# One matmul for both parts of an operand, and a state-space scan in two blocks of 128 steps

## The chip, the cores and the metric
The kernel runs on one core of a Trainium2 chip. The metric is the device time of one execution in microseconds, the median of three runs. A profile of one more execution was taken.

## The reference
One decoder block over 256 tokens of 2048 features, in float32: a mixer of two parallel branches, merged by sigmoid gates, and a mixture of 32 experts behind it. The parts that matter here:

```python
proj = rms_norm(x) @ w_in            # 2048 -> 512 (s5) + 1536 (lru x) + 1536 (lru y) + 2 * 2048 (gates)
bu = einsum('gpc,blgc->blgp', b_bar, u)                  # s5: 32 groups of 16 inputs, 64 complex states
states = scan(s[t] = lam_bar * s[t-1] + bu[t])           # over the 256 steps
y = real(einsum('gcp,blgp->blgc', c, states)) + d * u    # then gelu, and a sigmoid gate (w_glu)
h = scan(a[t] * h[t-1] + b[t]) * gelu(y_lru)             # lru: a and b from the conv of x_lru, by heads
merged = g_s5 * (out_s5 @ w_proj_s5) + g_lru * (out_lru @ w_proj_lru)
x = x + merged @ w_out               # then the experts, and a final norm
```

## The kernel before, in words
**Layout.** Features stand on the 128 partitions and the 256 tokens on the free axis, so a product of the mixer is a 128 x 256 tile, accumulated over 16 (w_in), 12 (w_plru) or 4 (w_ps5, w_glu) steps of k in one bank of PSUM. To keep float32's precision with the faster fp32r type, weights and activations are split into a high and a low part: `split` (L93) makes `hi` on ScalarE (L99) and `lo = raw - hi` on VectorE (L100), for 1024 columns at a time, and `mm3` (L103) issues three matmuls for each k: hi x hi, hi x lo, lo x hi. The activations' parts are `hT_hi` and `hT_lo` for the normalised input, and `br_hi`, `br_lo` for the branches' outputs (and, before the norm is known, for the raw input).

**Order of the work.** `in_unit` (L398) loads one 128-column unit of w_in (1 MB), splits it in two halves and issues 48 matmuls. The loop at L570 runs over 4 triples of heads: three units for y (GELU, L579), then for each head a unit for x, the head itself (`lru_head`: conv, two small products, gates) and one gate unit (`gate_lru`, tanh on ScalarE, L568). `lru_tail` ends a triple with the scan (L560) and writes `br` (L562, L563). Behind the first two triples stand state-space chunks 0 and 1 (`s5_chunk`, L409), then chunk 2, the last four gate units and chunk 3. Then come 16 units of w_plru (L602), which need the `br` of all heads; 16 units of the s5 gates (L613); the GLU of the state-space output (L624); w_ps5 (L651), whose products are gated (L662), added to the other branch on GpSimd (L663) and split (`merge`, L645: ScalarE, then VectorE L649); and w_out (L726, `mm3w`, 512-column matmuls with their own weight loads). The experts' stage behind it streams 201 MB of weights. The order on each engine is written out by a planner that simulates the program with costs of its own; `high_priority` puts the splits and the evacuations ahead of the state space. On the chip each engine runs its list in order.

**A state-space chunk.** It has four tiles of 128 states (two groups of 64), one after the other in pairs (`SB = 2`). For each tile two matmuls bring the inputs in (L422; 32 rows of contraction, float32, so each is two passes in the trace), at the row tile given by `tile_position`, into one `mid` bank. VectorE turns them by the angle of the step within a block of 16 (L430 to L435), scans all 16 blocks at once (L444), carries between blocks with 16 small instructions (L453 to L475) and adds the carry (L476, L477), scans again, and turns back (L483 to L488). Two matmuls for each tile form the output (L493; 32 columns, at the column tile 32q of the bank `yps[c]`), and L495 adds the skip term.

**Banks.** PSUM has eight: four `acc`, two `mid` (chunks, heads and two of the first y units), two `aux` (`yps` and small products). Of the SBUF pool `mp`, `bz`, `gz` and `st` have two buffers.

Of the kernel before, what the change touches and what calls it, by code (L numbers as in the profile page):

```python
# [35 lines left out]
def block_kernel(  # L36
# [323 lines left out]
    def powers(tc_, ts_):  # L360
# [20 lines left out]
    powers(blk_c, blk_s)
    rho16 = t16("rho16")
    V.tensor_tensor(rho16, rho, rho, op=ALU.mult)
    for _ in range(3):
        V.tensor_tensor(rho16, rho16, rho16, op=ALU.mult)
    d_loc = tb_.tile([P, 16, 16], F32, name="d_loc")
    d_blk = tb_.tile([P, 16, 16], F32, name="d_blk")
    V.tensor_copy(d_loc, rho[:, :, None].to_broadcast([P, 16, 16]))
    V.tensor_copy(d_blk, rho16[:, :, None].to_broadcast([P, 16, 16]))
    V.memset(d_loc[:, :, 0], 0.0)  # L390
    V.memset(d_blk[:, :, 0], 0.0)
# [6 lines left out]
    def in_unit(u, a_hi=hT_hi, a_lo=hT_lo, bank=acc_bank):  # L398
        raw = load_unit(w_in[u], 2048)
        ps = bank()[:, :T]  # L400
# [6 lines left out]
        return ps  # L407

    def s5_chunk(c):  # L409
        yps[c] = aux_bank()  # L410
        SB = 2
        for sb in range(4 // SB):
            bz = mp.tile([P, 2, SB, T], F32, tag="bz", bufs=2, name=nm("bz"))
            gz = mp.tile([P, 2, SB, T], F32, tag="gz", bufs=2, name=nm("gz"))
            s0 = 4 * c + sb * SB
            for i in range(SB):
                s = s0 + i
                q = s % 4
                rows = slice(32 * q, 32 * q + 32)
# [1 line left out]
                for ri in range(2):
                    PE.matmul(ps[:, ri * T:(ri + 1) * T], bt[rows, c, ri, :], uT[rows, c, :], start=True, stop=True,  # L422
                              tile_position=(32 * q, 0))
                p3 = ps.rearrange("p (r j t) -> p r j t", r=2, t=16)
                lc = loc_c[:, s, None, 0:16].to_broadcast([P, 16, 16])
                ls = loc_s[:, s, None, 0:16].to_broadcast([P, 16, 16])
                tt = mp.tile([P, 2, T], F32, tag="st", bufs=2, name=nm("st"))
                ttv = tt.rearrange("p r (j t) -> p r j t", t=16)
                bzv = bz[:, :, i, :].rearrange("p r (j t) -> p r j t", t=16)
                V.tensor_tensor(ttv[:, 0], p3[:, 1], ls, op=ALU.mult)  # L430
                V.tensor_tensor(ttv[:, 1], p3[:, 0], ls, op=ALU.mult)
                V.tensor_tensor(bzv[:, 0], p3[:, 0], lc, op=ALU.mult)
                V.tensor_tensor(bzv[:, 1], p3[:, 1], lc, op=ALU.mult)
                V.tensor_tensor(bz[:, 0, i, :], bz[:, 0, i, :], tt[:, 0], op=ALU.add)
                V.tensor_tensor(bz[:, 1, i, :], bz[:, 1, i, :], tt[:, 1], op=ALU.subtract)  # L435
            d3 = mp.tile([P, SB * T], F32, tag="d3", bufs=1, name=nm("d3"))
            A.activation(d3.rearrange("p (s j t) -> p s j t", s=SB, t=16),
                         d_loc[:, s0:s0 + SB, None, :].to_broadcast([P, SB, 16, 16]), AF.Copy)
            bz4 = bz.rearrange("p r s (j t) -> p r s j t", t=16)
            gz4 = gz.rearrange("p r s (j t) -> p r s j t", t=16)  # L440

            def scan():
                for ri in range(2):
                    V.tensor_tensor_scan(gz[:, ri].rearrange("p s t -> p (s t)"), d3,  # L444
                                         bz[:, ri].rearrange("p s t -> p (s t)"), 0.0, op0=ALU.mult, op1=ALU.add)

            scan()

            w = lambda: mp.tile([P, SB, 16], F32, tag="cw", bufs=8, name=nm("cw"))
            bc, bs = blk_c[:, s0:s0 + SB, 0:16], blk_s[:, s0:s0 + SB, 0:16]  # L450
            gr, gi = gz4[:, 0, :, :, 15], gz4[:, 1, :, :, 15]
            t1, t2, yr, yi, vr, vi = w(), w(), w(), w(), w(), w()
            V.tensor_tensor(yr, gr, bc, op=ALU.mult)  # L453
            V.tensor_tensor(t1, gi, bs, op=ALU.mult)
            V.tensor_tensor(yi, gi, bc, op=ALU.mult)
            V.tensor_tensor(t2, gr, bs, op=ALU.mult)
            V.tensor_tensor(yr, yr, t1, op=ALU.add)
            V.tensor_tensor(yi, yi, t2, op=ALU.subtract)
            fl = lambda t: t.rearrange("p s j -> p (s j)")
            db = fl(d_blk[:, s0:s0 + SB, :])  # L460
            V.tensor_tensor_scan(fl(vr), db, fl(yr), 0.0, op0=ALU.mult, op1=ALU.add)
            V.tensor_tensor_scan(fl(vi), db, fl(yi), 0.0, op0=ALU.mult, op1=ALU.add)
            bc, bs = blk_c[:, s0:s0 + SB, 1:16], blk_s[:, s0:s0 + SB, 1:16]
            v_r, v_i = vr[:, :, 0:15], vi[:, :, 0:15]
            t1, t2, yr, yi = w(), w(), w(), w()
            t1, t2, yr, yi = t1[:, :, 0:15], t2[:, :, 0:15], yr[:, :, 0:15], yi[:, :, 0:15]
            V.tensor_tensor(yr, v_r, bc, op=ALU.mult)
            V.tensor_tensor(t1, v_i, bs, op=ALU.mult)
            V.tensor_tensor(yi, v_i, bc, op=ALU.mult)
            V.tensor_tensor(t2, v_r, bs, op=ALU.mult)  # L470
            V.tensor_tensor(yr, yr, t1, op=ALU.subtract)
            V.tensor_tensor(yi, yi, t2, op=ALU.add)
            rb = rho[:, s0:s0 + SB, None].to_broadcast([P, SB, 15])
            V.tensor_tensor(yr, yr, rb, op=ALU.mult)
            V.tensor_tensor(yi, yi, rb, op=ALU.mult)  # L475
            V.tensor_tensor(bz4[:, 0, :, 1:16, 0], bz4[:, 0, :, 1:16, 0], yr, op=ALU.add)  # L476
            V.tensor_tensor(bz4[:, 1, :, 1:16, 0], bz4[:, 1, :, 1:16, 0], yi, op=ALU.add)  # L477
            scan()
            lc = loc_c[:, s0:s0 + SB, None, 0:16].to_broadcast([P, SB, 16, 16])
            ls = loc_s[:, s0:s0 + SB, None, 0:16].to_broadcast([P, SB, 16, 16])  # L480
            tr = mp.tile([P, SB, T], F32, tag="st", bufs=2, name=nm("so"))
            ti = mp.tile([P, SB, T], F32, tag="st", bufs=2, name=nm("so"))
            V.tensor_tensor(tr.rearrange("p s (j t) -> p s j t", t=16), gz4[:, 1], ls, op=ALU.mult)  # L483
            V.tensor_tensor(ti.rearrange("p s (j t) -> p s j t", t=16), gz4[:, 0], ls, op=ALU.mult)
            V.tensor_tensor(bz4[:, 0], gz4[:, 0], lc, op=ALU.mult)
            V.tensor_tensor(bz4[:, 1], gz4[:, 1], lc, op=ALU.mult)
            V.tensor_tensor(bz[:, 0], bz[:, 0], tr, op=ALU.subtract)
            V.tensor_tensor(bz[:, 1], bz[:, 1], ti, op=ALU.add)  # L488
            for i in range(SB):
                s = s0 + i  # L490
                q = s % 4
                for ri in range(2):
                    PE.matmul(yps[c][32 * q:32 * q + 32, :T], cp[:, s, ri, :], bz[:, ri, i, :],  # L493
                              start=(ri == 0), stop=(ri == 1), tile_position=(0, 32 * q))
# [631 lines left out]
```

## Time and profile before
| | us |
|---|---|
| median of 3 runs (lowest, highest) | 1090.77 (1089.81, 1092.85) |
| the profiled execution | 1093.92 |
| its span, first to last instruction | 1092.1 |
| TensorE (PE) busy | 994.2 |
| VectorE (DVE) busy | 645.6 |
| ScalarE (ACT) busy | 379.1 |
| GpSimd (POOL) busy | 75.6 |

The granted TensorE clock is 0.963 of full speed in the mean. Busy time is the union of an engine's instructions; an instruction's own time is longer than its distance to the next, since they overlap in the pipeline. Stretches are counted from the start of the span.

### The profile page before, as it was taken

What the parts mean: (1) busy time and instruction counts of PE and PEld (TensorE: products, weight loads), DVE (VectorE), ACT (ScalarE), POOL (GpSimd) and SP (SyncE); (2) the same over time, 40 slices, a digit from 0 to 9 for tenths busy, and PEclk for the clock granted to TensorE, in tenths of its full rate; (3) what the DMA queues carried; (4) which work ended last, traced back from release to release, by engine and by line L of the source; (5) the groups of instructions that cost most, each with busy time, mean ns of one, the idle gap of its engine ahead of it and who ended that gap; (6) DMA issues with size and microseconds to landing.
All of it is one profiled execution on the core that took longest, in us unless ns stands there. A gap on an engine that the chain in (4) does not pass through costs nothing. (4 is left out here: it accounts for less than half of the span.)

```text
span 1092.1 us, 18171 instructions
## 1 busy us (share of the span) xinstructions
PE 994.2 (91%) x7435; PEld 749.4 (69%) x7435; DVE 645.6 (59%) x1356; ACT 379.1 (35%) x591; POOL 75.6 (7%) x76
## 2 busy tenths in 40 slices
PE   5999999999999999999999999999988979797872
PEld 5999899998989999998889945445443424343220
DVE  7899999999999964458544433333333312232225
ACT  5568547577633354445434110111110101011102
POOL 4001201223200000006000000000000000000000
PEclk9999999999999999999999999989998989999897
DMA  7655444454244555554979699999999999999991
GB/s 274 212 171 201 155 158 151 157 178 165 97 147 158 184 190 191 193 182 166 392 290 373 247 393 419 375 419 420 419 419 420 419 420 418 420 420 419 420 383 80
DMA packets 45164, 308.93 MB, mean 283 GB/s; under 512 B 5040, under 2 KB 6736, under 8 KB 9744
## 3 DMA queue, kind: packets, MB, share of 16 engines
q1 hardware_dynamic: 44784, 306.84, 72.5%
q8 instruction: 60, 0.98, 0.4%
q0 software_dynamic: 288, 0.85, 0.4%
q14 instruction: 32, 0.26, 0.1%
HBM read 305.57 MB, written 2.10 MB: 282 GB/s over the span
## 5 line engine op out<-in xcount | busy, mean ns | idle before, releaser
L100 DVE TENSOR_TENSOR wlo<-raw,whi 128x1024 fp32r<-128x1024 f32 (+1 forms) x194 | 230.2, 1189 | 98.0 <-ACT whi L99 97.6
L99 ACT ACTIVATE whi<-raw 128x1024 fp32r<-128x1024 f32 (+1 forms) x194 | 197.5, 1022 | 226.8 <-PE acc L105 163.5
L106 PE MATMUL acc<-hT_hi,wlo 128*128 128x256 f32 x848 | 238.8, 282 | 0.0
L105 PE MATMUL acc<-hT_lo,whi 128*128 128x256 f32 x848 | 238.8, 282 | 0.0
L104 PE MATMUL acc<-hT_hi,whi 128*128 128x256 f32 x848 | 238.2, 282 | 0.0
L990 DVE TENSOR_TENSOR once<-acc,once 128x512 f32<-128x512 f32 x128 | 79.8, 685 | 141.0 <-PE acc L986 141.0
L105 PEld LDWEIGHTS acc<-hT_lo,whi 128*128 128x128 f32 x848 | 159.6, 188 | 2.6 <-issue 2.6
L106 PEld LDWEIGHTS acc<-hT_hi,wlo 128*128 128x128 f32 x848 | 159.5, 188 | 2.1 <-issue 2.1
L104 PEld LDWEIGHTS acc<-hT_hi,whi 128*128 128x128 f32 x848 | 159.2, 188 | 2.4 <-issue 2.4
L104 PE MATMUL acc<-br,whi 128*128 128x256 f32 x336 | 95.9, 291 | 8.1 <-ACT br L177 7.7
L105 PE MATMUL acc<-br,whi 128*128 128x256 f32 x336 | 96.8, 290 | 2.4 <-DVE br L178 2.2
L106 PE MATMUL acc<-br,wlo 128*128 128x256 f32 x336 | 96.0, 290 | 2.2 <-DVE wlo L100 2.2
L986 PE MATMUL acc<-ysb,sct 32*128 32x512 f32 x512 | 95.9, 682 | 1.5 <-DVE once L990 0.8
L942 PE MATMUL mid<-eraw,once 128*32 128x512 f32 x512 | 66.0, 632 | 23.8 <-DMA eraw<-in_w_exp_dram 23.8
L918 PEld LDWEIGHTS aux<-sel,x 128*128 128x128 f32 x512 | 61.0, 195 | 31.0 <-issue 20.8
L974 PE MATMUL mid<-eraw,act 128*32 128x512 f32 x504 | 67.8, 658 | 10.2 <-DVE act L955 8.2
L942 PE MATMUL mid<-eraw,xTe 128*32 128x512 f32 x488 | 61.1, 616 | 16.5 <-DMA eraw<-in_w_exp_dram 16.5
L104 PEld LDWEIGHTS acc<-br,whi 128*128 128x128 f32 x336 | 65.7, 198 | 10.0 <-ACT br L177 7.7
L945 ACT ACTIVATE gus<-mid 128x512 f32<-128x512 f32 x32 | 19.1, 597 | 153.6 <-PE mid L942 153.6
L918 PE MATMUL aux<-sel,x 128*128 128x128 f32 x512 | 67.5, 285 | 5.3 <-DVE sct L967 5.3
L105 PEld LDWEIGHTS acc<-br,whi 128*128 128x128 f32 x336 | 66.1, 197 | 4.4 <-DVE br L178 2.7
L106 PEld LDWEIGHTS acc<-br,wlo 128*128 128x128 f32 x336 | 65.8, 197 | 4.0 <-DVE wlo L100 2.4
(352 smaller groups left out, 1307.0 us busy)
## 6 DMA issues: line engine op xcount, KB each, us to landing
eraw<-in_w_exp_dram SPq DMA_DIRECT2D x188, 1024.0 KB, 19.9
raw<-in_w_in_dram SPq DMA_DIRECT2D x59, 1024.0 KB, 4.9
raw<-in_w_out_dram SPq DMA_DIRECT2D x16, 1024.0 KB, 6.3
raw<-in_w_plru_dram SPq DMA_DIRECT2D x16, 768.0 KB, 4.2
raw<-in_w_ps_dram SPq DMA_DIRECT2D x4, 1024.0 KB, 5.0
once<-in_w_exp_dram SPq DMA_DIRECT2D x4, 1024.0 KB, 9.1
xt<-in_xT_dram SPq DMA_DIRECT2D x4, 512.0 KB, 8.7
x<-in_x_dram SPq DMA_DIRECT2D x2, 1024.0 KB, 7.5
```

The lines of the kernel that those rows point to most:

```text
L99: A.activation(hi[:, :n], src, AF.Copy)
L100: V.tensor_tensor(lo[:, :n], src, hi[:, :n].bitcast(F32), op=ALU.subtract)
L104: PE.matmul(ps, whi, ahi, start=first, stop=False)
L105: PE.matmul(ps, whi, alo, start=False, stop=False)
L106: PE.matmul(ps, wlo, ahi, start=False, stop=last)
L918: PE.matmul(pt[:, kk * P:(kk + 1) * P], x1[h][:, k * P:(k + 1) * P], sel[b][:, h].rearrange("p e s -> p (e s)"), start=h == 0, stop=h == 1)
L942: mm = PE.matmul(ps[S * q:S * q + S, :], xT[e // B][:, 4 * j + q, es_], raw[:, q * 512:(q + 1) * 512], start=j == 0, stop=j == 3, tile_pos ...
L945: A.activation(gus[e], ps, AF.Copy)
L974: PE.matmul(ps[S * nb:S * nb + S, :], act[e][:, S * f:S * f + S], raw[:, bank(nb)], start=f == 0, stop=f == 1, tile_position=(0, S * nb))
L986: PE.matmul(sc[nb], sct[e][rows, h, :], ysb[e][rows, :], start=e == ex[0], stop=e == ex[-1], tile_position=(S * nb, 0))
L990: V.tensor_tensor(yacc[h][:, bank(nb)], sc[nb], old[:, bank(nb)], op=ALU.add)
```

## The change
It has these parts:
- `mm2` takes the place of `mm3` for w_in, w_plru and w_ps5. The two parts of the activation are read by one matmul (512 columns, into the two halves of a bank), and the low part of the weight by a second (256 columns, into the first half). The halves are added by `both`, a reduction on VectorE that reads PSUM and writes SBUF, before what reads the product: 88 times (12 y, 12 x, 16 gates, 16 w_plru, 16 s5 gates, 16 w_ps5).
- A chunk handles its four tiles together, in two blocks of 128 steps in place of sixteen of 16. The angles of 128 steps are worked out by six instructions (`fc`, `fs`); one scan per block and part replaces the two rounds; one carry stands between the blocks.
- The input matmuls go two tiles at a time into a tile of two banks (`two_banks`), part outside and state inside; the output ones likewise with four states inside.
- The banks are now four `acc`, one `two` and two `aux`; the heads' product moves from `mid` to `aux`. The pool is closed before the GLU and opened anew with `mid`. In SBUF, `bz`, `gz`, `st`, `d3` have one buffer.

```diff
+    def mm2(ps, whi, wlo, a2, first, last):
+        PE.matmul(ps, whi, a2, start=first, stop=False)
+        PE.matmul(ps[:, :T], wlo, a2[:, 0, :], start=False, stop=last)
+
+    def both(dst, ps):
+        V.tensor_reduce(dst, ps.rearrange("p (w t) -> p t w", w=2), axis=AX.X, op=ALU.add)
...
-    def in_unit(u, a_hi=hT_hi, a_lo=hT_lo, bank=acc_bank):
+    def in_unit(u, a2=hT2, bank=acc_bank):
...
-                mm3(ps, hi[:, cs_], lo[:, cs_], a_hi[k], a_lo[k], k == 0, k == KD - 1)
+                mm2(ps, hi[:, cs_], lo[:, cs_], a2[k], k == 0, k == KD - 1)
...
+        V.tensor_tensor(f4(fc), lc, bc, op=ALU.mult)
+        V.tensor_tensor(tt, ls, bs, op=ALU.mult)
+        V.tensor_tensor(f4(fc), f4(fc), tt, op=ALU.subtract)
+        V.tensor_tensor(f4(fs), ls, bc, op=ALU.mult)
+        V.tensor_tensor(tt, lc, bs, op=ALU.mult)
+        V.tensor_tensor(f4(fs), f4(fs), tt, op=ALU.add)
+        d3 = mp.tile([P, SB, HT], F32, tag="d3", name=nm("d3"))
+        A.activation(d3, rho[:, gs_, None].to_broadcast([P, SB, HT]), AF.Copy)
+        G.memset(d3[:, :, 0], 0.0)
...
+        for i0 in range(0, SB, 2):
+            tt = t4()
+            pair = two_banks()
+            for ri in range(2):
+                for i in (i0, i0 + 1):
+                    rows = slice(32 * i, 32 * i + 32)
+                    at = (i - i0) * 512 + ri * T
+                    PE.matmul(pair[:, at:at + T], bt[rows, c, ri, :], uT[rows, c, :], start=True, stop=True,
+                              tile_position=(32 * i, 0))
+            for i in (i0, i0 + 1):
+                p3 = pair[:, (i - i0) * 512:(i - i0 + 1) * 512].rearrange("p (r j t) -> p r j t", r=2, t=HT)
+                V.tensor_tensor(tt[:, :, i - i0, :].rearrange("p r (j t) -> p r j t", t=HT), p3,
+                                fs[:, None, None, i, :].to_broadcast([P, 2, 2, HT]), op=ALU.mult)
+                V.tensor_tensor(bz[:, :, :, i, :].rearrange("p j r t -> p r j t"), p3,
+                                fc[:, None, None, i, :].to_broadcast([P, 2, 2, HT]), op=ALU.mult)
+            for ri in range(2):
+                o = bz[:, :, ri, i0:i0 + 2, :]
+                V.tensor_tensor(o, o, tt[:, 1 - ri].rearrange("p s (j t) -> p j s t", t=HT), op=ALU.subtract if ri else ALU.add)
+        for j in range(2):
+            for ri in range(2):
+                V.tensor_tensor_scan(f2(gz[:, j, ri]), f2(d3), f2(bz[:, j, ri]), 0.0, op0=ALU.mult, op1=ALU.add)
+            if j == 0:
...
+        for j in range(2):
+            tt = t4().rearrange("p r s t -> p (r s t)").rearrange("p (r s t) -> p r s t", r=2, s=SB)
+            V.tensor_tensor(tt, gz[:, j], fs[:, None].to_broadcast([P, 2, SB, HT]), op=ALU.mult)
+            V.tensor_tensor(bz[:, j], gz[:, j], fc[:, None].to_broadcast([P, 2, SB, HT]), op=ALU.mult)
+            for ri in range(2):
+                o = bz[:, j, ri]
+                V.tensor_tensor(o, o, tt[:, 1 - ri], op=ALU.add if ri else ALU.subtract)
+        for ri in range(2):
             for i in range(SB):
...
+                PE.matmul(yps[c][32 * i:32 * i + 32, :T], cp[:, SB * c + i, ri, :], bz[:, :, ri, i, :],
+                          start=(ri == 0), stop=(ri == 1), tile_position=(0, 32 * i))
...
+            xi = lt("xi")
+            both(xi, ps_in)
...
-        ps = mid_bank()
+        ps = aux_bank()
...
-            A.activation(part[:, d, :], ps, AF.Tanh, bias=hcol(C_BGATE, 16 + d), scale=0.5)
+            both(part[:, d, :], ps)
+            A.activation(part[:, d, :], part[:, d, :], AF.Tanh, bias=hcol(C_BGATE, 16 + d), scale=0.5)
...
+    mixer_banks.close()
+    psum[0] = ctx.enter_context(tc.tile_pool(name="psum2", bufs=1, space=PSUM))
...
-                    mm3(ps, hi[:, cs_], lo[:, cs_], br_hi[k], br_lo[k], k == 0, k == 3)
...
+                    mm2(ps, hi[:, cs_], lo[:, cs_], br2[k], k == 0, k == 3)
+                tg = mp.tile([P, T], F32, tag=("fc", "fs")[dd], name=nm("tg"))
+                both(tg, ps)
+                V.scalar_tensor_tensor(tg, gs5[:, d, :], 1.0, tg, op0=ALU.add, op1=ALU.mult)
```

## Rows read from the trace of the kernel before

**Rows 1.** The page: busy us of each engine, share of the span, instructions

```profile
PE 994.2 (91%) x7435; PEld 749.4 (69%) x7435; DVE 645.6 (59%) x1356; ACT 379.1 (35%) x591; POOL 75.6 (7%) x76
```

**Rows 2.** Stages: length, busy of PE, PEld, DVE, ACT, POOL (instructions), clock, DMA share, GB/s

```profile
45.00:301.00 256.00, 251.95 (x2028) 240.87 (x2027) 248.16 (x595) 168.00 (x258) 43.90 (x36) 1.00 0.48 162
...
45.00:310.00 265.00, 258.77 (x2082) 247.21 (x2080) 257.15 (x611) 171.20 (x263) 43.90 (x36) 1.00 0.48 162
...
310.00:390.00 80.00, 80.00 (x609) 73.99 (x609) 76.42 (x168) 28.22 (x34) 0.00 (x0) 0.98 0.49 159
390.00:482.00 92.00, 92.00 (x769) 90.69 (x769) 42.52 (x38) 43.30 (x52) 0.00 (x0) 1.00 0.56 194
...
488.00:513.00 25.00, 22.41 (x183) 22.04 (x182) 20.52 (x41) 12.06 (x23) 14.78 (x16) 0.99 0.37 127
...
640.00:1065.00 425.00, 370.00 (x2721) 171.20 (x2714) 130.91 (x297) 45.77 (x96) 0.54 (x1) 0.94 1.00 414
```

**Rows 3.** Line L563, the heads' last: ns min/median/max, first and last start

```profile
L563 DVE TENSOR_TENSOR br<-pb,br x12: 392/416/609, 118.0 to 300.5; 128x256 fp32r<-128x256 f32 x12
```

**Rows 4.** Waits of PE up to 620 us: us in total, times, longest

```profile
PE aux L493 <- DVE bz L487: 2.6, 2, 2.2
PE acc L109 <- ACT whi L99: 2.4, 1, 2.4
```

**Rows 5.** Timeline of ACT, s5 gates: start, us, what (fourteen evenly spaced rows, outer two)

```profile
401.34 0.45 ACT L616 ACTIVATE gs<-acc,half_b 128x256 f32<-128x256 f32 x1
...
475.39 0.46 ACT L616 ACTIVATE gs<-acc,half_b 128x256 f32<-128x256 f32 x1
```

**Rows 6.** Timeline of PE, w_out: the first and last of five rows

```profile
521.90 0.39 PE L109 MATMUL acc<-whi,br 128*128 128x512 f32 x1
...
522.81 0.39 PE L110 MATMUL acc<-whi,br 128*128 128x512 f32 x1
```

**Rows 7.** PE: groups of tiled passes in the timeline; then all by form

```profile
341.04 1.12 PE L422 MATMUL mid<-uT,bt 32*128 32x256 f32 x4
...
284.14 1.14 PE L422 MATMUL mid<-uT,bt 32*128 32x256 f32 x8
...
335.89 0.62 PE L493 MATMUL aux<-bz,cp 128*32 128x256 f32 x2
...
337.23 1.06 PE L493 MATMUL aux<-bz,cp 128*32 128x256 f32 x6
...
722.37 1.92 PE L974 MATMUL mid<-eraw,act 128*32 128x512 f32 x16 [0.47 <-DVE act L955]
...
L422 PE MATMUL mid<-uT,bt 32*128 32x256 f32 x64 | 15.8, 400 | 0.0
...
L493 PE MATMUL aux<-bz,cp 128*32 128x256 f32 x64 | 13.9, 396 | 2.6 <-DVE bz L487 2.6
```

**Rows 8.** Timeline of DVE in chunk 3: two 512-column instructions in a row

```profile
358.65 0.69 DVE L483 TENSOR_TENSOR so<-gz,loc_s 128x512 f32<-128x512 f32 x1
359.25 0.69 DVE L484 TENSOR_TENSOR so<-gz,loc_s 128x512 f32<-128x512 f32 x1
```

**Rows 9.** DVE by line and form: busy us, mean ns, idle before

```profile
L444 DVE TENSOR_TENSOR_SCAN gz<-d,bz 128x512 f32<-128x512 f32 x32 | 39.2, 1261 | 0.0
...
L967 DVE COPY sct<-aux 128x256 f32<-128x256 f32 x32 | 13.4, 418 | 0.0
...
L483 DVE TENSOR_TENSOR so<-gz,loc_s 128x512 f32<-128x512 f32 x8 | 5.5, 685 | 0.0
...
L470 DVE TENSOR_TENSOR cw<-cw,blk_s 128x30 f32<-128x30 f32 x8 | 1.5, 183 | 0.0
```

**Rows 10.** Timeline around the end of w_ps5: PE, DVE, PE

```profile
510.04 0.28 PE L106 MATMUL acc<-br,wlo 128*128 128x256 f32 x1
...
511.76 0.41 DVE L662 SCALAR_TENSOR_TENSOR tg<-gs,acc 128x256 f32<-128x256 f32 x1
...
512.71 0.80 PE L109 MATMUL acc<-whi,br 128*128 128x512 f32 x1 [2.39 <-ACT whi L99]
```

More of the change, by code (lines that the diff above doesn't have):

```diff
@@ L64, in block_kernel @@
     units = [mixer_units.enter_context(tc.tile_pool(name="units", bufs=1, reuse_waits="tile")), 4]
-    psum = ctx.enter_context(tc.tile_pool(name="psum", bufs=1, space=PSUM))
+    mixer_banks = ExitStack()
+    psum = [mixer_banks.enter_context(tc.tile_pool(name="psum", bufs=1, space=PSUM))]
     uid = [0]
@@ L73, in acc_bank, with two_banks @@
     def acc_bank():
-        return psum.tile([P, 512], F32, tag="acc", bufs=4, name=nm("acc"))
+        return psum[0].tile([P, 512], F32, tag="acc", bufs=4, name=nm("acc"))
     def mid_bank():
-        return psum.tile([P, 512], F32, tag="mid", bufs=2, name=nm("mid"))
+        return psum[0].tile([P, 512], F32, tag="mid", bufs=2, name=nm("mid"))
+    def two_banks():
+        return psum[0].tile([P, 1024], F32, tag="two", bufs=1, name=nm("two"))
     def aux_bank():
-        return psum.tile([P, 512], F32, tag="aux", bufs=2, name=nm("aux"))
+        return psum[0].tile([P, 512], F32, tag="aux", bufs=2, name=nm("aux"))
     ident = const.tile([P, P], F32, name="ident")
@@ L133, in block_kernel @@
     br_lo = [br[k // 4][:, 1, k % 4, :] for k in range(KD)]
-    hT = [hp.tile([P, KD, T], F32R, name=f"hT_{w}") for w in ("hi", "lo")]
-    hT_hi, hT_lo = ([t[:, k, :] for k in range(KD)] for t in hT)
+    br2 = [br[k // 4][:, :, k % 4, :] for k in range(KD)]
+    hT = hp.tile([P, 2, KD, T], F32R, name="hT")
+    hT_hi, hT_lo = ([hT[:, w, k, :] for k in range(KD)] for w in range(2))
+    hT2 = [hT[:, :, k, :] for k in range(KD)]
     part = hp.tile([P, KD, T], F32, name="part")
@@ L363, in powers @@
         n = 1
-        while n < 16:
+        while n < top:
             bc = tc_[:, :, n:n + 1].to_broadcast([P, 16, n])
@@ L376, in powers @@
             n *= 2
-    powers(loc_c, loc_s)
+    powers(loc_c, loc_s, 16)
     V.tensor_copy(blk_c[:, :, 1], loc_c[:, :, 16])
     V.tensor_copy(blk_s[:, :, 1], loc_s[:, :, 16])
[L381 to L391, printed above, removed]
+    powers(blk_c, blk_s, 8)
+    hop_c = tb_.tile([P, 16], F32, name="hop_c")
+    hop_s = tb_.tile([P, 16], F32, name="hop_s")
+    V.tensor_tensor(hop_c, rho, blk_c[:, :, 8], op=ALU.mult)
+    V.tensor_tensor(hop_s, rho, blk_s[:, :, 8], op=ALU.mult)
     wks.close()
@@ L405, in in_unit @@
                 cs_ = slice(kk * P, (kk + 1) * P)
-                mm3(ps, hi[:, cs_], lo[:, cs_], a_hi[k], a_lo[k], k == 0, k == KD - 1)
+                mm2(ps, hi[:, cs_], lo[:, cs_], a2[k], k == 0, k == KD - 1)
         return ps
+    SB, HT = 4, T // 2
     def s5_chunk(c):
         yps[c] = aux_bank()
[L411 to L415, printed above, removed]
-            for i in range(SB):
-                s = s0 + i
-                q = s % 4
-                rows = slice(32 * q, 32 * q + 32)
-                ps = mid_bank()
[L421 to L494, printed above, removed]
@@ new lines, in s5_chunk @@
+        gs_ = slice(SB * c, SB * c + SB)
+        fc = mp.tile([P, SB, HT], F32, tag="fc", name=nm("fc"))
+        fs = mp.tile([P, SB, HT], F32, tag="fs", name=nm("fs"))
+        t4 = lambda: mp.tile([P, 2, SB // 2, T], F32, tag="st", name=nm("st"))
+        tt = t4().rearrange("p r s t -> p (r s t)")[:, 0:SB * HT].rearrange("p (s j t) -> p s j t", s=SB, t=16)
+        f4 = lambda f: f.rearrange("p s (j t) -> p s j t", t=16)
+        sh = [P, SB, HT // 16, 16]
+        lc, ls = (l[:, gs_, None, 0:16].to_broadcast(sh) for l in (loc_c, loc_s))
```

54 lines of the change are left out of this document (35 added, 19 removed).

## The prediction, made blind
> **What bounds the kernel now.** I read the page first, then the stages, then the waits, then single instructions. TensorE is busy in 91% of the span [rows 1]. The table by stage [rows 2] cuts the span where the work changes. From 45 to 310 us the input matmuls of the conv and gate units run, with the recurrence's heads and the first state-space chunks beside them: TensorE is busy for 258.8 of 265 us, but VectorE for 257.2 too. Up to 301 us, where the last head has written the operand of the next stage [rows 3], VectorE has 248.2 of 256. So the first stage has two full engines. From 310 to 390 (w_plru) TensorE is full and VectorE at 76 of 80, because chunks 2 and 3 of the state space are worked off there; from 390 to 482 (s5 gates) TensorE is full and VectorE at 42.5 of 92. The stage of w_ps5 (488 to 513) has VectorE at 20.5 of 25. From 640 to 1065 the experts run at a DMA share of 1.00 and 414 GB/s: that stage lasts as long as its bytes, so whatever the mixer gains or loses moves it as a block. After the start TensorE hardly waits in the mixer: two waits of L493 for VectorE, 2.6 us together, and one of 2.4 us for ScalarE ahead of w_out are among the longest [rows 4].
>
> **Matmuls in pairs of parts.** A step of k is three 256-column matmuls now; it becomes one of 512 columns over both parts and one of 256. An s5-gate unit is 48 of the old matmuls, and its evacuations follow each other by 74.05 us in 13 steps [rows 5], 5.70 us a unit, so 118.7 ns a matmul. The 512-column ones of w_out, also with a weight load each, follow each other by 0.91 us in 4 steps [rows 6]: 227 ns. A step costs 356 ns now, and 227 + 119 = 346 ns after: 10.4 ns saved, from which I take that each matmul has a fixed part. 56 input units of 16 steps, 16 w_plru units of 12 and 16 w_ps5 units of 4 are 1152 steps: **-12.0 us**, of which 6.7 lie in the 40 units before w_plru, 4.7 in w_plru and the s5 gates, 0.7 in w_ps5. The bounds: nothing, if 512 columns cost twice 118.7, and -18 us, if the 256-column matmul beside it also falls by some 5 ns. The row is the nearest there is: same operand type, same weight load.
> The Trainium skill ("TensorE: Matmul & The Clock Gate", section "Wait — 56ns, not 53.3ns?") puts the fixed cost of a warm matmul at about 2.5 ns, by which 1152 matmuls fewer would save an estimated 2.9 us; the rows above say 10.4 ns a step.
>
> **State-space matmuls.** The input side (L422) stands on row tiles. A group of four passes takes 1.12 us, and where the order happened to bring two states into two banks, eight passes take 1.14 us [rows 7]. The 64 passes are 12 groups of four and 2 of eight, 15.7 us. After: 8 groups of eight, 9.1 us, **-6.6 us**. The output side (L493) is a group of two (0.62 us) and one of six (1.06 us) for each half chunk, 8 x 1.68 = 13.4 us. With the part outside and the state inside, four column tiles go at once: sixteen 512-column passes of that kind take 1.92 us [rows 7], and 256 columns should take some 1.1 us, 1.4 if the group is cut in two. Four groups: 4.4 to 5.6 us, **-8.5 us**. Together 15.1, of which about 9.5 before 310 us (two and a half chunks).
>
> **VectorE.** Instructions overlap: two 128x512 ones start 0.60 us apart though each is busy 0.69 [rows 8, 9], so I count busy time less 0.09. Half a chunk now: 12 of 256 columns (0.33, as L967), 4 scans (1.17, L444), 18 small (0.1, as L470), 6 of 512 (0.60, L483), in all 14.1 us; a chunk 28.6 with its last addition. After: 6 instructions for the tables, 12 to turn in, 4 to turn out, all of 512 (13.2), 4 of 1024 (4.6), 4 scans (4.7), the carry (0.5), the last addition: 23.4. A chunk saves 5.2 us. The tables of constants lose 14 small instructions and gain 2, -1.3 us.
> Against that stand 88 new reductions (`both`), 512 columns from PSUM to 256. No row shows one. Bounds: 0.42 us, if outputs count (a 256-column copy from PSUM, L967), 1.26 us, if each element passes twice as in the scan (L444) [rows 9]. I take 0.69 busy, 0.60 net, the row of 512 elements read once (L483), since a reduction reads 512. The ScalarE readers then read SBUF, at the same cost.
> First stage, up to the last head: 248.2, less 10.4 (two chunks), less 1.3, plus 40 x 0.60 = 24, less about 9.7 for chunk 2's share there, which can be put off into w_plru: 250.8, and with the 7.8 us in which VectorE idles now, 258.6. The last head would be done at 303.6. TensorE by itself would be through at 310 - 6.7 - 9.5 = 293.8. So VectorE decides there, and **+10 us** of TensorE's saving is lost, between 0 (the idle time shrinks, chunk 1 is put off too) and 16 (chunk 2 is not put off). Behind it, from 310 to 482, VectorE had 118.9 us; it gets 9.7 + 32 x 0.60 = 29 more and 10.4 less, 138 of the some 162 TensorE needs: covered by the s5 gates, where VectorE idles half the time.
>
> **w_ps5.** For one d VectorE now has half a split (0.57), one addition and one merge (0.33 each), 1.23 us against TensorE's 1.42; it gets 0.60 more and becomes the longer one, 29.3 us for 16 d against 22. Now its last L662 starts at 511.76, 1.7 us after TensorE's last matmul there, and w_out's first matmul at 512.71 waits behind the merges on ScalarE [rows 4, 10]. w_out needs two free banks, so the evacuation of the 14th d: about 14 x 1.83 + 2 = 27.6 us after the start (2 for the first product), where 16 x 1.42 and the wait of 2.4, 25.1 us, are taken now. With w_out's first splits queued behind these on VectorE I take **+4 us**, between 0 and 10.
>
> **Banks and queues.** The mixer's banks are closed before the GLU, so its first matmul waits for the last reduction of the s5 gates: **+1.3 us** (0.69 and two hand-overs), 0 to 3. A head's product moves from a `mid` bank to an `aux` bank, and a chunk's output holds the other: the second head of a triple waits until the chunk is done, where before it waited for the chunk's last `mid` bank. I cost that at nothing: TensorE has gate and conv units to go on with; without them it would be 2 to 5 us. One `two` tile instead of two `mid` banks makes the second pair wait for four reads, 2.4 us, under matmuls of other units. The memset on POOL queues behind the heads' products there, VectorE's scan behind it: four times, under 1 us each, at nothing. No DMA is added, SP's queue is unchanged.
>
> **The sum**: -12.0 - 15.1 + 10 + 4 + 1.3 = -11.8 us. The profiled execution took 1093.92 us with a span of 1092.1, so 1082.1 after; the median of the runs shown is 3.2 below it, 1090.77 - 11.8 = **1079 us**.
>
> **Rivals.** (a) VectorE does not bind: reductions nearer 0.42, or the order hides more. For it: VectorE's state-space work has slack until the GLU, at 482. Then some -26: 1065 us. Against: 248 of 256 us now.
> (b) The 512-column matmul is no cheaper. Then TensorE is through with the first stage at 300.5, still under VectorE's 303.6, and only the 5.4 us behind it are lost: -6.4, 1084 us. Against: the rows at 227 ns. By the 2.5 ns that the Trainium skill gives ("TensorE: Matmul & The Clock Gate", the section above) the time would be near this.
> (c) VectorE becomes the bound of the whole mixer, slower than before. One mechanism: the reduction's own time, in the first stage and w_ps5. 56 of them lie where VectorE decides, so -11.8 turns to zero at 0.21 us more each, a reduction of 0.90 us. At the scan's 1.26 us it is 56 x 0.57 = 32 more: +20, 1111 us. For it: no reduction of this shape is in the trace, and its pairs lie 1 KB apart. Against: all elementwise rows cost the same per element, from PSUM or SBUF.
> The Trainium skill ("TensorEngine Tiling (Array Packing)", section "PSUM Bottleneck") warns of just this side: tiling speeds up TensorE and not the evacuation, which may become the bottleneck.
> (d) It all cancels: chunk 2 is not put off and w_ps5 costs 8: near 1090. That the tiles don't overlap as said is excluded by the rows of eight passes.
>
> **How the numbers follow.** My forecast, 1070 to 1087: 0.46. (a) 0.15. (b) lies with the forecast's upper part, 0.07 beside it. (d) 0.14, (c) 0.18. The measurement tells 0.3%, 3.3 us, from no change. Faster: 0.46 + 0.15 + 0.05 = 0.66 (a little of (b) ends within 0.3%), same 0.16, slower 0.18. The range leaves out half of (c) and the end of (a): 1062 to 1096.
>
> **What would show it.** Right: 512-column matmuls 227 ns apart; an s5-gate unit 5.53 us; groups of eight at 1.14 us and of sixteen near 1.1; reductions of 0.69 us; VectorE without gaps up to about 300 us and TensorE waiting there for some 10 us; w_out starting 5 us or more behind the last w_ps5 matmul. Wrong: TensorE as full as now before w_plru (then (a)), reductions of 0.9 us or more (then (c)), or an expert stage that does not keep its length.

## The result, and the profile after

The changed kernel takes **1126.0 us** (1123.6 to 1128.4) against 1091.8 for the kernel before on the same chip: a ratio of 1.031, 95% interval 1.028 to 1.034. The forecast was 1079, its range ended at 1096. The profiled execution took 1128.4 with a span of 1126.7 us.

The page's busy times, and the stages (length; busy of PE, PEld, DVE, ACT, POOL; clock, DMA share, GB/s), to be held against [rows 1, 2]:

```profile
PE 990.9 (88%) x6283; PEld 695.6 (62%) x6283; DVE 674.2 (60%) x1252; ACT 372.2 (33%) x581; POOL 70.1 (6%) x80
...
45.00:341.00 296.00, 263.04 (x1484) 222.73 (x1483) 286.42 (x566) 165.60 (x255) 39.43 (x40) 0.93 0.43 147
341.00:409.00 68.00, 62.15 (x352) 53.48 (x351) 54.49 (x78) 27.12 (x32) 0.00 (x0) 0.95 0.51 172
409.00:501.00 92.00, 92.00 (x526) 80.67 (x525) 52.44 (x51) 40.98 (x48) 0.00 (x0) 1.00 0.57 191
...
275.00:300.00 25.00, 15.94 (x81) 12.38 (x80) 25.00 (x45) 13.46 (x23) 5.66 (x5) 0.76 0.36 116
325.00:350.00 25.00, 15.17 (x74) 12.47 (x75) 24.10 (x44) 10.65 (x17) 5.16 (x6) 0.73 0.23 66
```

The last head, and the chunks' ends (ns min/median/max, first and last start), against [rows 3]:

```profile
L561 DVE TENSOR_TENSOR br<-pb,br x12: 392/408/413, 177.2 to 340.9; 128x256 fp32r<-128x256 f32 x12
...
L490 DVE SCALAR_TENSOR_TENSOR uT<-uT,prm,aux x4: 464/468/481, 194.2 to 364.8; 128x256 f32<-128x256 f32 x4
```

The waits of PE from 45 to 410 us (us in total, times, longest), against [rows 4]:

```profile
PE acc L114 <- DVE part L119: 13.7, 4, 6.4
PE aux L108 <- ACT xh L533: 6.1, 1, 6.1
PE acc L114 <- DVE pl L119: 5.3, 1, 5.3
PE two L453 <- DVE bz L459: 4.9, 1, 4.9
PE acc L115 <- DVE wlo L104: 3.2, 4, 1.8
```

The last head comes at 340.9 us in place of 300.5, with VectorE busy for 286.4 of the 296 us before it and TensorE waiting, most of all for the reductions (L119). Between 275 and 300 us VectorE fills all 25 us and TensorE 15.9, at a mean granted clock of 0.76. The four chunks, by contrast, end earlier, at 364.8 against 395.6. The s5 gates run at full TensorE again (92 of 92), but their end has moved, and w_out's first matmul stands at 537.9 in place of 512.7 [rows 10]:

```profile
L122 PE MATMUL acc<-whi,br x160: 278/389/632, 537.9 to 640.6; 128*128 128x512 f32 x96, 128*128 128x256 f32 x64
```

The parts that the change is made of, one by one. Reductions (with the counts of the whole kernel), steps of `mm2`, tiled groups, and the tanh of the s5 gates:

```profile
L119 DVE TENSOR_REDUCE part<-acc x26: 657/678/691, 58.1 to 339.2; 128x256 f32<-128x512 f32 x26
L119 DVE TENSOR_REDUCE gs<-acc x16: 690/691/692, 417.1 to 501.4; 128x256 f32<-128x512 f32 x16
...
419.75 0.40 PE L114 MATMUL acc<-hT,whi 128*128 128x512 f32 x1
419.98 0.28 PE L115 MATMUL acc<-hT,wlo 128*128 128x256 f32 x1
420.10 0.40 PE L114 MATMUL acc<-hT,whi 128*128 128x512 f32 x1
...
126.86 1.13 PE L453 MATMUL two<-uT,bt 32*128 32x256 f32 x8
...
191.83 1.07 PE L488 MATMUL aux<-bz,cp 128*32 128x256 f32 x16
...
L620 ACT ACTIVATE gs<-gs,half_b x16: 493/494/497, 418.0 to 502.3; 128x256 f32<-128x256 f32 x16
```

A reduction takes 0.68 to 0.69 us, eight and sixteen tiled passes 1.13 and 1.07 us: as forecast. An s5-gate unit takes 84.3 / 15 = 5.62 us, where 5.53 were forecast and 5.70 were there before. None of this explains 35 us; the question was where they come from.

### The profile page after: what moved, and what is told of

Same layout as the page of the kernel before. It is cut to its first block, busy times and chain, and to the rows that moved or that the text cites. A ratio compares the mean times of both kernels' runs of the same rounds, so it can differ in the third digit from the quotient of the medians.

```text
span 1126.7 us, 15795 instructions
## 1 busy us (share of the span) xinstructions
PE 990.9 (88%) x6283; PEld 695.6 (62%) x6283; DVE 674.2 (60%) x1252; ACT 372.2 (33%) x581; POOL 70.1 (6%) x80
## 5 line engine op out<-in xcount | busy, mean ns | idle before, releaser
L114 PE MATMUL acc<-hT,whi 128*128 128x512 f32 x848 | 307.5, 402 | 12.8 <-DVE part L119 7.3
L103 ACT ACTIVATE whi<-raw 128x1024 fp32r<-128x1024 f32 (+1 forms) x194 | 197.0, 1022 | 237.6 <-PE acc L114 139.8
L115 PE MATMUL acc<-hT,wlo 128*128 128x256 f32 x848 | 243.1, 288 | 2.7 <-DVE wlo L104 2.7
L114 PEld LDWEIGHTS acc<-hT,whi 128*128 128x128 f32 x848 | 163.1, 193 | 51.8 <-ACT pb L587 5.1
L115 PEld LDWEIGHTS acc<-hT,wlo 128*128 128x128 f32 x848 | 163.5, 193 | 5.5 <-DVE wlo L104 4.5
L114 PE MATMUL acc<-br,whi 128*128 128x512 f32 x272 | 99.4, 407 | 16.4 <-DVE part L119 6.4
L114 PEld LDWEIGHTS acc<-br,whi 128*128 128x128 f32 x272 | 52.7, 194 | 30.2 <-issue 15.8
L995 PEld LDWEIGHTS acc<-ysb,sct 32*128 32x128 f32 x512 | 40.7, 194 | 35.3 <-issue 26.7
L986 ACT ACTIVATE ysb<-mid 128x512 f32<-128x512 f32 x32 | 19.1, 597 | 129.8 <-PE mid L983 129.8
L122 PE MATMUL acc<-whi,br 128*128 128x512 f32 (+1 forms) x160 | 57.0, 357 | 1.5 <-DVE tg L119 1.5
L124 PE MATMUL acc<-wlo,br 128*128 128x512 f32 (+1 forms) x160 | 55.4, 359 | 2.2 <-DVE wlo L104 2.2
```

Of the source, the lines that this page charges most:

```text
L103: A.activation(hi[:, :n], src, AF.Copy)
L114: PE.matmul(ps, whi, a2, start=first, stop=False)
L115: PE.matmul(ps[:, :T], wlo, a2[:, 0, :], start=False, stop=last)
L995: PE.matmul(sc[nb], sct[e][rows, h, :], ysb[e][rows, :], start=e == ex[0], stop=e == ex[-1], tile_position=(S * nb, 0))
```

## The experiments

The theories at the start: **A**, the heads' product shares the `aux` banks with the constants' transposes and the chunks' outputs and comes late (the first head's tanh is at 132 us, at 86 before); **B**, VectorE is full, and every reduction ahead of the last head delays it; **C**, `pl` (the reduced w_plru product) sits in the chunks' single `fc` and `fs` buffers, so w_plru can't be evacuated while a chunk is under way. Later came **D**, the place of chunks 2 and 3 in VectorE's order. Times of whole kernels are medians, beside runs of the kernel before (1093.6 to 1094.8 us in these comparisons); a stage or a place in the span comes from the one profiled execution of each kernel. A miss is a time outside the range of the theory under test.

### The two halves of the change alone

`e2_mm2_only`: two-part matmuls and reductions put into the kernel before. `e3_s5_only`: the changed kernel without them:

```diff
     def mm2(ps, whi, wlo, a2, first, last):
-        PE.matmul(ps, whi, a2, start=first, stop=False)
-        PE.matmul(ps[:, :T], wlo, a2[:, 0, :], start=False, stop=last)
+        mm3(ps[:, :T], whi, wlo, a2[:, 0, :], a2[:, 1, :], first, last)
...
-            both(xi, ps_in)
```

> The kernel before with the two-part matmuls and their 88 reductions alone: old state space, old banks with the heads in mid. Theory A (banks): the heads start early as before, at some 82 us; VectorE is loaded by 40 x 0.6 = 24 us more before the last br without the 12 us that the new chunks save, so the last br comes some 15 to 20 us later than 300 and the time is 1095 to 1110 us, faster than the changed kernel. Theory B (VectorE): worse than the changed kernel, 1130 us or more, since VectorE lacks the saving of the new state space.

> The changed kernel with three matmuls per step again and no reductions: new state space and new banks alone. Theory A (banks): most of the loss stays, the first head starts near 130 us, the last br comes after 325 us, time 1105 to 1120 us. Theory B (VectorE): VectorE has 5 us less per chunk than before and no reductions, so the last br comes before 300 us and the time is 1075 to 1088 us.

Measured: e2 **1120.7 us**, ratio 1.025 (1.019 to 1.031); e3 **1084.4 us**, 0.992 (0.990 to 0.995). Their first stages up to the last head, and the last head, e2 first, then e3:

```profile
45.00:325.70 280.70, 264.51 (x1431) 219.95 (x1430) 268.42 (x623) 170.35 (x258) 38.65 (x36) 0.96 0.44 149
...
L577 DVE TENSOR_TENSOR br<-pb,br x12: 409/413/426, 133.2 to 325.4; 128x256 fp32r<-128x256 f32 x12
```

```profile
45.00:301.30 256.30, 251.38 (x2084) 243.64 (x2083) 248.15 (x503) 162.55 (x255) 50.75 (x40) 1.00 0.50 167
...
L553 DVE TENSOR_TENSOR br<-pb,br x12: 409/413/417, 165.0 to 301.0; 128x256 fp32r<-128x256 f32 x12
```

The loss is in the two-part matmuls. In e2 the last head is 25 us late, what 40 reductions take (24 us); its time is a miss for both theories, between 1110 and 1130. In e3 the heads are in `aux` as in the changed kernel, and their first tanh is at 118 us, yet the last head is on time: theory A falls. B holds in kind. But e3 gains only 9 us, and its last head is no earlier than before, though VectorE has less to do for a chunk: by 301 us it has already worked off almost all of chunk 2 (it ends at 307, at 340 before).

### The heads' bank

```diff
-        ps = aux_bank()
+        ps = acc_bank()
         for w in range(2):
```

> The changed kernel with one edit: the heads' product takes an acc bank in place of an aux bank. Theory A (banks): the heads queue in the aux banks behind the transposes of the constants and behind the chunks' outputs, so the first head starts at 130 us in place of 82 and the last br is written at 341 us in place of 300. Then the first head should start near 85 us, the last br come at 305 to 315 us and the time fall by 20 to 30 us, to 1096 to 1106 us. Theory B (VectorE is full with the 88 reductions, whatever the banks): the last br stays at 330 us or later, and the time at 1120 us or more.

> The changed kernel with two edits: the heads' product in an acc bank, and the reduced w_plru product in two buffers of its own in place of the chunks' fc and fs. Theory C: because fc and fs have one buffer each, w_plru's evacuation can't begin before chunk 3 is done, so the chunk can't lie under w_plru and the s5 gates. Then this kernel is faster than the one with the heads' product in an acc bank alone by 3 us or more, and chunk 3 ends after the first w_plru evacuation. If the tag does not matter the two agree within 1 us.

Measured: **1184.4 us**, 1.085 (1.079 to 1.091), and **1184.0 us** with `pl` in own buffers as well (its diff stands further below). Both are misses, for A and for C; only B's "1120 us or more" holds, and B has no reason for so much. Chunks' ends, the last head and the longest waits of the first:

```profile
L490 DVE SCALAR_TENSOR_TENSOR uT<-uT,prm,aux x4: 449/474/480, 154.3 to 282.8; 128x256 f32<-128x256 f32 x4
...
L561 DVE TENSOR_TENSOR br<-pb,br x12: 409/414/958, 158.1 to 395.0; 128x256 fp32r<-128x256 f32 x12
...
PE two L453 <- DVE bz L459: 27.5, 4, 10.9
PE acc L108 <- ACT xh L533: 26.8, 11, 6.2
PE aux L488 <- DVE bz L485: 18.0, 2, 9.3
```

With the heads out of `aux`, the written order has all four chunks ended at 282.8, and the last head comes 54 us later still, at 395.0. TensorE's order has chunk matmuls and heads close behind their operands, and TensorE waits for them 72.3 us in these three rows. So the `aux` bank had not delayed the heads. That it had held the chunks back, and that this had helped, is inferred from the order and has no run of its own; by amount e1 has only 7.5 us more chunk work ahead of its last head than the changed kernel (96.3 against 88.8), so most of the 54 us are waits. This is what led to D. Theory C could not show here, since no chunk is left when w_plru starts.

### Reductions only behind, or only ahead of, the last head

```diff
-    def in_unit(u, a2=hT2, bank=acc_bank):
+    def in_unit(u, a2=hT2, bank=acc_bank, mm=mm2o):
...
-        ps = in_unit(28 + d)
+        ps = in_unit(28 + d, mm=mm2)
```

`mm2o` is `mm3` with `mm2`'s operands; this is `f2_mm2_late` (w_ps5 has `mm2o` too). `f3_mm2_early` has it the other way round.

> The changed kernel with the two-part matmuls only in w_plru and the s5 gates, where VectorE has room; three matmuls per step elsewhere, w_ps5 among it. Theory B: the 56 reductions ahead of the last head and in w_ps5 make the whole loss, the 32 others are hidden. Then the time is that of the new state space alone (1084.4 us) less up to 4.7 us: 1079 to 1085 us. If the reductions cost wherever they stand: 1090 us or more.

> The changed kernel with the two-part matmuls only in the 40 units ahead of the last head; three matmuls per step in w_plru, the s5 gates and w_ps5. Theory B: the 40 reductions there keep most of the loss: the last br at 330 to 341 us, and 1112 to 1126 us. If the loss sits in w_plru (evacuation tied to chunk 3) or in w_ps5: below 1105 us.

Measured: f2 **1099.4 us**, 1.003 (1.000 to 1.006), a miss; f3 **1122.2 us**, 1.023 (1.020 to 1.026), as B says. f2's first stage equals e3's (last head at 301.2), but then TensorE waits, and the first product of w_plru is used at 334.6 us (L615):

```profile
PE acc L114 <- DVE pl L119: 16.6, 1, 16.6
...
L615 DVE SCALAR_TENSOR_TENSOR part<-part,pl x16: 417/424/426, 334.6 to 388.5; 128x256 f32<-128x256 f32 x16
```

The first reduction of w_plru writes into `fc`, which the chunk still needs. That is C.

### Holding chunks 2 and 3 back

`f1_chunks_late` (on the changed kernel) and `f4_late_both` (on f2); `pl` in `fc` and `fs` makes sure that a chunk can't start before the unit ahead of it:

```diff
-    s5_chunk(2)
...
-    s5_chunk(3)
     for d in range(KD):
...
+        if d in (1, 8):
+            s5_chunk(2 if d == 1 else 3)
```

> The changed kernel with chunks 2 and 3 moved behind the second and the ninth unit of w_plru; they reuse the buffers of the reduced w_plru products, so they can't start before. Theory D (order): in the changed kernel chunk 2 and most of chunk 3, some 40 us of VectorE, stand ahead of the last head; only 24 of the 40 us by which the last br is late are the 40 reductions. Then the last br comes at 300 to 312 us, the chunks are hidden by w_plru and the s5 gates, and the time is 1090 to 1103 us. Theory B alone (reductions): the last br stays within 8 us of 341 and the time within 8 us of 1126. Rival: the chunks don't end before the GLU, and the loss turns up there; then the last br is early and the first matmul of w_out still later than 525 us.

> The kernel with two-part matmuls only in w_plru and the s5 gates, and with chunks 2 and 3 moved behind the second and the ninth unit of w_plru. Theory D: VectorE is then relieved of some 20 us before the last head, TensorE decides there, and the last br comes at 285 to 297 us in place of 301; time 1065 to 1080 us, the fastest so far. If the order does not matter: as with the chunks where they were, within 3 us.

Measured: f1 **1128.0 us**, 1.029 (1.026 to 1.032); f4 **1104.4 us**, 1.008 (1.005 to 1.011). Both times are misses, though the last head moves nearly as D says, from 340.9 to 313.7 and from 301.2 to 291.9. What was gained is given back in w_plru: f1's w_out starts at 542.2 us, as late as the rival said, but not for its reason, since the chunks end at 406.5, ahead of the GLU. f1's wait in w_plru:

```profile
PE acc L114 <- DVE pl L119: 25.0, 2, 14.2
```

### Both repairs together

`pl` gets two buffers of its own; where chunks are held back, only units 0 and 11 share `fc`, with the chunks behind them:

```diff
-        pl = mp.tile([P, T], F32, tag=("fc", "fs")[d % 2], name=nm("pl"))
+        pl = gsp.tile([P, T], F32, tag="pl", bufs=2, name=nm("pl"))
```

> Two-part matmuls only in w_plru and the s5 gates, as in the run that gave 1099.4 us, with the reduced w_plru product in two buffers of its own. There TensorE waited 16.6 us in one piece for the first reduction of w_plru, which may only write into fc when the last chunk is done with it. Theory C (the shared buffers): this wait goes, the first w_plru evacuation comes at 306 us in place of 335 and the time falls by 12 to 20 us, to 1079 to 1087 us. If the reductions themselves were the cost: within 4 us of 1099.

> As the previous kernel, with chunks 2 and 3 held back behind the first and the twelfth unit of w_plru (those two units alone share the chunk's buffer). With the chunks held back before, the last br came at 291.9 us in place of 301.2, but TensorE waited 26.7 us for the shared buffers. Theories C and D together: last br near 292 us, no wait above 5 us in w_plru, time 1068 to 1078 us. If holding the chunks back only moves the load: 1079 to 1087 us, as the previous kernel.

> The changed kernel with the reduced w_plru product in two buffers of its own, nothing else. Theory C: the first w_plru evacuation comes right behind the last br (341 us) in place of 359, TensorE's wait of 5.3 us goes, and the time falls by 8 to 15 us, to 1111 to 1118 us. If the buffers don't matter there, since chunk 3 is nearly done by then: within 3 us of 1126.

> The changed kernel, two-part matmuls everywhere, with both repairs: w_plru's reduced product in its own buffers but for the first and the twelfth unit, behind which chunks 2 and 3 are held back. Theories C and D: the last br near 314 us, no long wait in w_plru, the time 1095 to 1105 us; what then remains against the kernel before is the 40 reductions ahead of the last head (24 us, less the saving of the chunks) and w_ps5. If the time stays above 1115 us, the reductions of w_plru and the s5 gates are not hidden after all.

Measured:

| | mm2 in | `pl` own | chunks 2, 3 late | us | ratio to before | last head | w_out starts |
|---|---|---|---|---|---|---|---|
| the changed kernel | all | no | no | 1126.0 | 1.031 (1.028 to 1.034) | 340.9 | 537.9 |
| g3 | all | yes | no | 1115.6 | 1.019 (1.015 to 1.022) | 340.4 | 530.6 |
| g4 | all | yes | yes | 1100.6 | 1.007 (1.004 to 1.010) | 312.6 | 510.4 |
| g1 | w_plru, s5 gates | yes | no | 1073.9 | 0.981 (0.979 to 0.984) | 301.1 | 493.6 |
| g2 | w_plru, s5 gates | yes | yes | **1069.9** | 0.979 (0.977 to 0.982) | 288.1 | 490.7 |

g2, g3 and g4 came within their expected ranges, g1 5 us below its range. In g1 the wait of 16.6 us is gone, and the first product of w_plru is used at 308.6 us, 26 us earlier than in f2:

```profile
L615 DVE SCALAR_TENSOR_TENSOR part<-part,pl x16: 391/409/419, 308.6 to 373.2; 128x256 f32<-128x256 f32 x16
```

Last head and first stage of g4, then of g2:

```profile
L561 DVE TENSOR_TENSOR br<-pb,br x12: 405/408/411, 176.9 to 312.6; 128x256 fp32r<-128x256 f32 x12
...
45.00:313.00 268.00, 247.78 (x1429) 212.76 (x1428) 254.38 (x513) 162.96 (x253) 42.40 (x39) 0.97 0.47 162
```

```profile
L562 DVE TENSOR_TENSOR br<-pb,br x12: 408/414/954, 165.1 to 288.1; 128x256 fp32r<-128x256 f32 x12
...
45.00:288.00 243.00, 240.52 (x2002) 234.21 (x2001) 225.40 (x467) 157.24 (x249) 49.07 (x39) 1.00 0.50 170
```

In g2 TensorE is full up to the last head (240.5 of 243) and VectorE is not (225.4). It is the fastest kernel of the study, though its interval and g1's overlap. What VectorE had to do for the chunks ahead of the last head, in the changed kernel (45 to 341.3 us) and in g4 (45 to 313 us); columns: count, busy us, mean ns, idle before:

```profile
L467 DVE TENSOR_TENSOR_SCAN gz<-d,bz 128x512 f32<-128x512 f32 x14 | 19.0, 1383 | 0.0
L457 DVE TENSOR_TENSOR st<-two,fs 128x512 f32<-128x512 f32 x16 | 10.8, 676 | 0.0
...
L485 DVE TENSOR_TENSOR bz<-bz,st 128x512 f32<-128x512 f32 x12 | 9.3, 813 | 0.0
...
L481 DVE TENSOR_TENSOR st<-gz,fs 128x1024 f32<-128x1024 f32 x6 | 7.3, 1211 | 0.0
```

```profile
L467 DVE TENSOR_TENSOR_SCAN gz<-d,bz 128x512 f32<-128x512 f32 x8 | 10.9, 1396 | 0.0
...
L485 DVE TENSOR_TENSOR bz<-bz,st 128x512 f32<-128x512 f32 x8 | 6.2, 812 | 0.0
...
L457 DVE TENSOR_TENSOR st<-two,fs 128x512 f32<-128x512 f32 x8 | 5.4, 680 | 0.0
...
L481 DVE TENSOR_TENSOR st<-gz,fs 128x1024 f32<-128x1024 f32 x4 | 4.9, 1213 | 0.0
```

The whole kernel has 16 of the scans, 16 of L457, 16 of L485 and 8 of L481. In the changed kernel all four chunks have been turned in, and three turned out, before the last head; in g4 two chunks and no more. Over all lines of `s5_chunk`, each instruction counted from the end of the one before it, that is 88.8 us of VectorE against 50.7, and the kernel before had 71.8 there. The 38 us less bring the last head 28 us earlier, not 38: VectorE's busy time falls by 32.0 us, since other work takes some of the place, and it idles for 4.0 us more (13.6 of 268, 9.6 of 296).

### The price of a reduction, and w_ps5

On g4: `h1_ps5_mm3` has `mm3` and no reduction in w_ps5, `h2_twice` does each of the 40 early reductions twice, `h3_half` lets ScalarE copy one half:

```diff
+    def half(dst, ps):
+        A.activation(dst, ps[:, :T], AF.Copy)
+        V.tensor_tensor(dst, dst, ps[:, T:], op=ALU.add)
...
-            both(xi, ps_in)
+            half(xi, ps_in)
```

> The repaired changed kernel (1100.6 us) with three matmuls per step and no reductions in w_ps5. If w_ps5's reductions cost what the prediction said, 4 us between 0 and 10: 1092 to 1099 us, and the wait of TensorE between its last w_ps5 matmul and w_out shrinks. If w_ps5 costs nothing: within 2 us of 1100.6.

> The repaired changed kernel with each of the 40 reductions ahead of the last head done twice. Theory B (VectorE decides there, one for one): 40 x 0.6 = 24 us more, 1118 to 1130 us, with the last br some 24 us later than 314. If another wait decides there: under 10 us more.

> The repaired changed kernel where ScalarE copies the first half of the 40 products ahead of the last head out of PSUM and VectorE adds the second half, 256 columns in place of a reduction over 512. Theory B: VectorE saves about 0.27 us each, 11 us, and the time is 1086 to 1094 us. Rival: the extra hand-over between ScalarE and VectorE ahead of each head costs as much as it saves: 1097 to 1108 us.

Measured: h1 **1090.7 us**, 0.997 (0.995 to 0.999); h2 **1123.0 us**, 1.026 (1.021 to 1.030); h3 **1097.6 us**, 1.004 (1.002 to 1.006). h2's last head, then h3's first stage:

```profile
L562 DVE TENSOR_TENSOR br<-pb,br x12: 407/410/415, 186.8 to 332.6; 128x256 fp32r<-128x256 f32 x12
```

```profile
45.00:312.60 267.60, 245.56 (x1397) 210.33 (x1396) 239.26 (x506) 178.42 (x293) 41.92 (x39) 0.96 0.46 156
```

h2: 40 more reductions make the last head 20.0 us later and the time 22.4 us longer, 0.56 us each. h3 takes 15 us of busy time off VectorE (239.3 against 254.4), and the last head stays where it was (312.2 against 312.6): VectorE now idles instead, in kind what the rival with the extra hand-over said. So in g4 the amount of VectorE's work alone no longer sets the last head; that the hand-over takes its place is not shown. h3's w_out even starts 4.8 us later than g4's (515.2 against 510.4), so its shorter time comes from behind that point.

h1 is 10.0 us faster than g4, a little beyond the 9 allowed. From the last tanh of the s5 gates to w_out's first matmul it needs 32.8 us (477.4 to 510.2) and g4 35.6 (474.8 to 510.4): w_ps5's reductions account for 2.8 us there. But since h1's last head is 3.7 us later (316.3), the two start w_out together, and the whole difference of the profiles lies behind it, where h1 takes 578.1 us and g4 592.8, although the code is the same (g4's profiled execution, 1104.9, was 4.3 us above its median). In f3, which has no reductions in w_ps5 either, this stretch is 590.4, in the kernel before 579.4, in g2 575.4. In g4 the DMA share is 0.77 between 670 and 710 us, in h1 0.97. Three stretches of 5 us in g4, in the columns of [rows 2]:

```profile
680.00:685.00 5.00, 5.00 (x14) 2.00 (x12) 0.69 (x1) 0.00 (x0) 0.00 (x0) 0.67 1.01 421
685.00:690.00 5.00, 5.00 (x13) 2.52 (x10) 1.29 (x2) 0.00 (x0) 0.00 (x0) 0.50 0.63 262
690.00:695.00 5.00, 4.64 (x18) 2.62 (x20) 2.45 (x6) 0.22 (x1) 0.00 (x0) 0.50 0.00 0
```

TensorE's granted clock falls to half while the engine is busy, and only then do the transfers stop. Just ahead of the fall and in it stand groups of passes with 32 rows of contraction (L994, four at 679.7 and eight at 682.2 us). The same dip, a mean clock of 0.79 and a DMA share of 0.77 in 40 us, stands in e2, f3 and h2, the three other kernels that need 590 us or so behind w_out's start (589.9 to 591.3); the changed kernel has a weaker one (0.91 and 0.90), and in g2 both are 1.00. The written order of TensorE's instructions in that stretch differs between these kernels. Whether that is the cause was not tried.

## Why the prediction was wrong

**The failed step** is in the paragraph on VectorE: "less about 9.7 for chunk 2's share there, which can be put off into w_plru". The forecast left some 52 us of chunk work ahead of the last head (71.8, less 10.4 and 9.7). In the changed kernel it was 88.8: chunk 2 was not put off, and most of chunk 3 came ahead of the last head too. The prediction's bound for that, 16 us, took the order of before as the worst case. By this account the 37 us more are the 37.3 us by which the last head comes later than forecast (340.9, not 303.6). g4 holds the chunks back: 50.7 us of chunk work there, the last head at 312.6, the time 15.0 us below g3. That bears out most of it, 28 us; the 9 us by which g4's last head is still later than 303.6, with no more chunk work than forecast, are other work of VectorE and 13.6 us of idle time where the forecast had 7.8. From the last head to w_out's first matmul the sum held, 197.3 us forecast (303.6 to 512.7 - 11.8) and 197.0 measured, but in part by luck: TensorE idles for 5.9 of the 68 us behind the last head, which was not foreseen, and finds chunk matmuls done that the forecast had placed there. What is left of the 47 us is 9.4 us behind w_out's start (588.8 against 579.4), the stretch whose cause is open.

**Not seen at all**: `pl` in the single buffers `fc` and `fs`. The prediction relied on chunks 2 and 3 being covered by w_plru and the s5 gates; with this tag they can't be, as w_plru's first reduction waits until the chunk is done with the buffer. Own buffers are worth 10.4 us on the changed kernel (g3), and 25.5 on f2 (g1); up to w_out's first matmul the profiles show 7.3 and 17.8 us of that (511.4 in f2). Holding the chunks back pays only with them: 1128.0 with shared buffers, 1115.6 with own ones alone, 1100.6 with both.

**VectorE's costs** were right: reductions at 0.69 busy and 24.4 us for 40 (24 forecast), a chunk at 24.1 us (96.3 for the four in e1, 23.4 forecast). So was what follows from them in kind, TensorE waiting for VectorE ahead of the last head. The reductions cost about what they take: the last head is 20.0 us later in h2, 25 in e2. That they would fit beside the saving on the chunks was not true even with chunks 2 and 3 behind the last head: g4 is at 1.007, its last head 12.1 us later than before.

**Two-part matmuls**: -12.0 forecast. The step is 351 ns (5.62 / 16), 512 columns 0.23 us and 256 columns 0.12; 5 ns a step saved, not 10.4, so 5 to 6 us for 1152 steps. The Trainium skill ("TensorE: Matmul & The Clock Gate", section "Wait — 56ns, not 53.3ns?") gives 2.5 ns for a matmul's fixed part; the saving here lies between that and the forecast. Even so they do no harm where VectorE has room: g1, with 32 reductions behind the last head, is at 0.981 and e3, without them, at 0.992. In the two profiles g1 is 3.8 us ahead at w_out's first matmul (493.6 against 497.4); 448 steps by 5 ns would be 2.3. The rest of the 10 us between the medians is not explained.

**State-space matmuls**: the groups took 1.13 and 1.07 us, as forecast; e3, with them and the new chunk, gains 0.8%, and its w_out starts 15.3 us earlier than before (497.4).

**w_ps5**: +4 forecast, 2.8 us measured up to w_out, up to 10.0 with the open part. The sign given for it did not come: w_out's first matmul is 1.8 us behind w_ps5's last (536.1 to 537.9), not 5 or more, as TensorE had already waited for the reductions among the matmuls of w_ps5 (3.1 us). The prediction also passed over that `mm2` needs the low part of the activation at once: w_ps5's matmuls wait 1.6 us for `br`'s low part (L645), where the kernel before had two waits of 0.6 us together.

**Banks**: closing the pool was put at +1.3 us; the GLU's first matmul waits 0.9 us for the last reduction. The single `two` tile was counted as covered; it costs one wait of 4.9 us (L453). **Heads in aux at nothing**: right, e3's last head is on time with them.

**Rivals.** (c) had the sign, by another way: its condition, a reduction of 0.90 us or more, was not met (0.69). (a) falls: VectorE binds, and TensorE is not "as full as now before w_plru" (263.0 of 296 us). (b) falls by half: the step did get cheaper, by half of what was said. (d) had named the mechanism, a chunk 2 that is not put off, but stopped at no change. Of the signs of being wrong, "an expert stage that does not keep its length" came true, and that part is open.

## What to carry to other kernels

Where one engine is full ahead of a point that others wait for, count not only what a change adds to it, but which deferrable work the order puts ahead of that point; a cheaper block of work may simply be placed earlier and cost more there. Work that can wait is best tied behind that point by a real dependency, and a buffer that early and late work share must not make the late work's first step wait for the deferred block. Moving work from a full engine to an idle one pays stage by stage: here the same two-part matmuls gained behind the last head, while ahead of it each reduction that they need cost some 0.56 us.

## What the runs showed that was not expected

- TensorE's waits were followed by slower work: in the two 25 us stretches above in which it was busy for 15.9 and 15.2 us, its mean granted clock was 0.76 and 0.73, between its two levels of 1.2 and 2.4 GHz, and some of its 512-column matmuls are busy for 0.63 us; in the s5 gates, where TensorE never pauses, the clock is 1.00 and they take 0.40.
- A step of one 512-column and one 256-column matmul takes 351 ns, three 256-column ones 356: one matmul less saved 5 ns, not 10.
- From w_out's first matmul to the end the profiles show 575 to 593 us with the same code; in the four longest the clock falls to half and the transfers stop, in that order. A few us between two medians can lie there, so the places of the last head and of w_out's first matmul tell more of the mixer than the time does.
